# Conditioning map of a four-layer diffusion step: where its two sums are formed, and beside which sub-layers

## The chip, the cores and the metric

The kernel runs on one core of a Trainium2 chip. The metric is device time in microseconds (us) of one execution; lower is better. The engines are the tensor engine (PE; PEld is its weight load), the vector engine (DVE), the scalar engine (ACT), GpSimd (POOL) and SyncE (SP), which issues the loads.

## What is computed

One step of a backbone of four layers over 128 context tokens and 512 latent tokens of 1024 channels, all in fp32. Each layer has a token mixer (latent attention, centred pooling, grouped 2-D Fourier, short gated convolution) and a gated ConvFFN. Both sub-layers are modulated by six vectors (shift, scale, gate) that come from a conditioning map:

```python
mod = jax.nn.silu(cond) @ P["ada_w"][li] + P["ada_b"][li]      # cond: c or c_ctx; ada_w: 1024 x 6144 per layer
sh1, sc1, g1, sh2, sc2, g2 = jnp.split(mod, 6, axis=-1)
h = _modulate(_rmsnorm(x, P["norm1_w"][li]), sh1, sc1)
x = x + g1[:, None, :] * mixer(h)
h = _modulate(_rmsnorm(x, P["norm2_w"][li]), sh2, sc2)
x = x + g2[:, None, :] * _conv_ffn(h, ...)
```

There are two conditioning vectors (one for context, one for latent tokens), so the map of a layer is a 2 x 1024 by 1024 x 6144 product whose 25 MB of weights are used once.

## The kernel before

Activations lie with channels on partitions: `x` is eight chunks of 128 channels by 640 tokens. Every fp32 product is three products of rounded parts (`wh`/`wl` for a weight and its rest, `XH`/`XL` or `hh`/`hl` for the operand). A weight comes as a 128 x 1024 tile (`wraw`), ACT casts it to `wh` (L184), DVE subtracts to get `wl` (L185). `mm3` (L225) then runs 48 matmuls of about 320 columns into a wide PSUM tile `mm`, of which there are two. In an FFN a unit is such a tile of weights: 44 products up and 24 down, in thirds. After a pair of products up, DVE evacuates both PSUM tiles (`ev`, L391), applies two taps of the convolution (`gc`, L412 and L413), forms `hd` (L452, L453) and its rest `hl` (L402). After a product down, DVE updates `x` (L362, L363).

The map is worked on in tiles of 128 input channels by 1024 outputs; a layer has 48, eight for a group of 1024 outputs, 192 in all. `ada_step` (L128) does one tile: it loads up to the pool's number of tiles ahead, but not past `ada["cap"]`, and then multiplies in one of two ways.

- **Direct** (where `ada["early"]` is None): four matmuls of the tile itself (`adaraw`) with the conditioning vectors as stationary operand (L160).
- **Sums** (where `ada["early"]` is a pool): the products are summed over the eight channel chunks beside the tensor engine, into two tiles `adasum` (`a0`, `a1`) of 128 x 1024, one per conditioning vector. After the eighth tile, eight small matmuls (L160, `pick`) add over the partitions. Then DVE transposes (L163) and adds the offset (L167).

Before, the tiles go so. Layer 0: 16 direct tiles at the start, one group of eight as sums in the projections (`three`, `krope`, `kv`), eight direct in `latent_keys`, 16 direct in the heads (one per stage of the 41 in `heads`). Layer 1: 48 as sums in FFN 0. Layer 2: 24 direct in the pooling mixer (three after each chunk, `proj` in `pool`), 24 as sums in FFN 1. Layer 3: 48 as sums in FFN 2. FFN 3 has none. An FFN calls `ada_step` after each unit up from the third on and after each product down of the first two thirds (58 calls).

Each engine runs its instructions in the order in which the framework's scheduler placed them when the program was built; a waiting instruction holds all that stand behind it on its engine. SP issues weight tiles and map tiles from one queue.

Of the kernel before, what the change touches and what calls it, by code (L numbers as in the profile page):

```python
# [13 lines left out]
ALU = mybir.AluOpType  # L14
# [40 lines left out]
# column offsets in the array of small per-channel vectors  # L55
# [18 lines left out]
def build(tc, a, plan=None):  # L74
# [53 lines left out]
    def ada_step(limit):  # L128
        i = ada["done"]
        end = min(limit, DEPTH) * 48  # L130
# [11 lines left out]
        if ada["sums"]:  # L142
            # the products summed over the channel chunks beside the tensor engine
            c_, (a0, a1) = [cond_s[:, k, r : r + 1] for r in range(2)], ada["sums"]
            if k == 0:
                V.tensor_scalar(a0, raw, c_[0], None, ALU.mult)
                S.activation(a1, raw, AF.Copy, scale=c_[1])
            else:
                V.scalar_tensor_tensor(a0, raw, c_[0], a0, ALU.mult, ALU.add)  # L149
                S.activation(raw, raw, AF.Copy, scale=c_[1])  # L150
                G.tensor_tensor(a1, a1, raw, ALU.add)  # L151
            todo = [(pick[:, r], acc, r == 0, r == 1) for r, acc in enumerate(ada["sums"])] if k == 7 else []
        else:
            todo = [(condz[:, k], raw, k == 0, k == 7)]
# [39 lines left out]
    def prefetch(upto):  # L194
        """emit the loads of the units up to the given count of weight units, but none beyond a barrier"""
# [27 lines left out]
    def mm3(o, wh, wl, mh, ml, n, bias, m=P, mid=None, apart=False):  # L223
        """o (token columns 192:832, bias columns 190:192) = sum over n chunks of w[k].T @ moving[k];
        mid: functions to call after a chunk; apart: the two banks one after the other"""  # L225
# [20 lines left out]
    st = dict(xh=None, xl=None, ssum=None, rstd=None, rB=None, xap=None, xstack=None)  # L246

    def norm_scale(l, which, lo):
        """per-channel factor norm_w * (1 + scale) of both condition vectors, four chunks"""
# [25 lines left out]
    def norm_prep(d, nxt):  # L275
        """after chunk d of x is final: its squares, and the modulated operand of sub-layer nxt = (layer, which)"""
        norm_sq(d, nxt is None)
        if nxt is not None:
            norm_xa(d, nxt)
# [41 lines left out]
    def rms_a(ssum, n, pool=None, rest=None):  # L321
        """rstd of the five token tiles, one value per partition"""
# [18 lines left out]
    def rms_b(r, pool=None, bufs=2):  # L341
        """rstd along the free dimension of every partition"""
# [45 lines left out]
    def evac(o, m=P):  # L388
        """psum * rstd with the two bias columns in front"""
# [15 lines left out]
    def conv3(gp, cols, bias):  # L405
        """three taps over the padded row (zeros at 0, 129, 642); outputs at 0:128 and 129:641"""
# [14 lines left out]
    def ffn(l, nxt):  # L421
# [49 lines left out]
        # a third of the products down follows the first products up of the next third  # L471
# [10 lines left out]
    def mla(nxt):  # L482
# [4 lines left out]
        def start():  # L487
# [18 lines left out]
            ada["cap"] = 32  # L506
# [43 lines left out]
        def take(dst, *parts):  # L550
            """normalise a projection, add its shift; parts: psum pieces, the two bias columns first"""
# [13 lines left out]
        def three(wh, wl):  # L565
            """the first three projections at once: their first four channel chunks while the shifts and scales of
            the others are still under way"""
# [15 lines left out]
            with tc.manual_schedule(engines={mybir.EngineType.PE}):  # L583
# [3 lines left out]
                ada["early"] = st["nb"]  # L587
# [9 lines left out]
                more(2)  # L597
# [4 lines left out]
            more(2)  # L602
# [13 lines left out]
        def krope(wh, wl):  # L616
            o = psum_mm()
            mm3(o, wh, wl, st["xh"], st["xl"], KC, True, m=96)
            more(2)
# [14 lines left out]
        def kv(i):  # L634
            def fn(wh, wl):
                o = psum_mm()
                mm3(o, wh, wl, st["xh"], st["xl"], KC, True, mid=None if i else {0: latent_q_stats, 4: latent_q})
                more(1)
# [5 lines left out]
        def heads_start():  # L644
            # the projections of the tokens are done: their operands make room for the heads
# [7 lines left out]
        def latent_keys():  # L653
            ada["early"] = None
            more(1)
# [5 lines left out]
            more(7)  # L661
# [11 lines left out]
        def heads_pools():  # L673
# [3 lines left out]
            ada["cap"] = 48  # L677
# [11 lines left out]
        # ---- the heads: scores of one query block beside the values of the block before, other  # L689
        # products in between ----  # L690
# [8 lines left out]
        def product(wh, wl, mh, ml, n, halves, post):  # L699
            """one output chunk, a half of the moving columns (one psum bank) at a time"""  # L700
# [100 lines left out]
        def combine(dst, o, n, hh, cols):  # L801
            """the two halves of the value operand: o[0:64] + o[64:128]"""
# [5 lines left out]
        class Block:  # L808
            """256 queries of one head"""
# [62 lines left out]
        class Context:  # L872
            """the prompt's own queries and keys, two heads"""
# [85 lines left out]
        def heads():  # L959
# [7 lines left out]
            # products to fit in beside the blocks: (first stage, weights, pieces, number of pieces)  # L967
# [30 lines left out]
            def fill(stage, k):  # L998
                """the next k pieces of the items open at this stage"""
# [25 lines left out]
            for i in range(len(blocks) + 1):  # L1025
# [4 lines left out]
                if i % nst == 0 and i:  # L1030
                    # the operands of the next pair must stand
# [105 lines left out]
    def pool(nxt):  # L1137
# [7 lines left out]
        def start():  # L1145
# [11 lines left out]
            cell["ada"] = ada["pool"], ada["bufs"]  # L1157
            ada["pool"], ada["bufs"], ada["cap"] = cell["pool"], 5, 2 * 48 + 24

        def finish():  # L1160
            ada["pool"], ada["bufs"] = cell["ada"]
            ada["cap"] = DEPTH * 48
            ctx.close()
# [35 lines left out]
        def proj(g):  # L1199
            def fn(wh, wl):  # L1200
# [7 lines left out]
                for i in range(2):  # L1208
                    finish_chunk(2 * g + i, cell["o"].pop(0))
                    for _ in range(3):  # L1210
                        ada_step(l + 2)
# [16 lines left out]
    def fourier(nxt):  # L1228
# [21 lines left out]
        def table(dst_h, dst_l, src):  # L1250
            """a constant table in its two parts"""
# [15 lines left out]
        def shift():  # L1267
            # the shift is constant over time: it reaches only the zero frequency
# [382 lines left out]
```

## Time and profile before

| | |
|---|---|
| runs | 2812.65, 2810.16, 2804.65 us; median 2810.16 |
| span of the profiled execution, first to last instruction | 2811.5 us; no separate time is given for it |
| PE busy | 2712.0 us (96%) |
| DVE busy | 1802.0 us (64%) |
| ACT busy | 1158.7 us (41%) |
| POOL busy | 549.6 us (20%) |

The page gives busy time by engine, the chain of waits that ended last, and groups of instructions. A share over the whole span is a mean over stages with different limits, so the trace is read by stage: windows (busy time in a stretch), waits (who waited for whom) and timelines (instructions in order of time).

### The profile page before, as it was taken

The page shows a single profiled execution, that of the slowest core. Times are in us where ns is not written, and L with a number is a line of the kernel's source. Part 1 is how long each engine was busy: PE and PEld are TensorE (multiplying, and loading weights), DVE is VectorE, ACT ScalarE, POOL GpSimd, SP SyncE. Part 2 cuts the span into 40 slices and gives each one's busy share as a digit, 9 for nine tenths or more (in the row PEclk, how much of TensorE's full clock was granted, in tenths as well). Part 3 has the DMA queues.
Part 4 walks back from the last instruction along what each step waited for, and adds up shares of the span by engine and source line. Part 5 has one row for each costly group of instructions (what it writes and reads, how often), then busy time and mean ns, then how long its engine had stood idle before and what let it go on. Part 6 is the DMA issues. An engine that isn't in the chain of part 4 may idle for free.

```text
span 2811.5 us, 44335 instructions
## 1 busy us (share of the span) xinstructions
PE 2712.0 (96%) x18417; PEld 2614.4 (93%) x18417; DVE 1802.0 (64%) x2354; ACT 1158.7 (41%) x1693; POOL 549.6 (20%) x328
## 2 busy tenths in 40 slices
PE   7999999999999889999999999999999999999998
PEld 5788989999999779999998999999999999999998
DVE  5778888877855888644454688686555555535353
ACT  4566665434433444332333354343332233313231
POOL 3222323422320333200012133332010010000001
PEclk9999999999999999999999999999999999999998
DMA  7431113443432544312221244433122221222221
GB/s 286 133 103 44 44 35 104 154 141 135 128 107 70 186 156 148 116 68 75 75 69 56 91 150 143 150 133 123 64 79 75 76 76 69 75 76 72 79 71 58
DMA packets 85656, 287.69 MB, mean 102 GB/s; under 512 B 10880, under 2 KB 13872, under 8 KB 85456
## 3 DMA queue, kind: packets, MB, share of 16 engines
q1 hardware_dynamic: 84816, 284.44, 30.0%
q8 instruction: 145, 2.38, 0.3%
q14 instruction: 55, 0.45, 0.1%
q10 hardware_dynamic: 288, 0.25, 0.0%
q0 software_dynamic: 352, 0.17, 0.0%
HBM read 279.42 MB, written 2.77 MB: 100 GB/s over the span
## 4 chain that ended last, share of the span: by engine, by line
PE 74%; DVE 14%; issue 5%; ACT 3%; DMA 2%; POOL 2%; SPq 0%; POOLq 0%; DVEq 0%; ACTq 0%
PE mm L235 62%; DVE adasum L149 4%; PE smp L708 3%; DVE wl L185 2%; DMA adaraw<-in_ada_w 2%; POOL adasum L151 2%; PE mm L823 1%; PE smp L845 1%; DVE ev L391 1%; DVE hl L402 1%; PE mm L1320 1%; PE adaacc L160 1%; DVE XL L312 1%; PE smp L861 1%; PE smp L754 1%
## 5 line engine op out<-in xcount | busy, mean ns | idle before, releaser
L235 PE MATMUL mm<-XH,wh 128*128 128x322 f32 (+1 forms) x3280 | 765.6, 315 | 34.1 <-DVE ev L391 29.2
L235 PE MATMUL mm<-XH,wl 128*128 128x322 f32 (+1 forms) x3280 | 760.8, 313 | 5.8 <-DVE wl L185 5.8
L235 PE MATMUL mm<-XL,wh 128*128 128x322 f32 (+1 forms) x3280 | 760.7, 313 | 1.5 <-DVE XL L312 1.5
L184 ACT CAST wh<-wraw 128x1024 fp32r<-128x1024 f32 (+4 forms) x355 | 348.4, 983 | 756.2 <-PE mm L235 639.7
L235 PEld LDWEIGHTS mm<-XH,wh 128*128 128x128 f32 (+1 forms) x3280 | 557.3, 191 | 45.9 <-issue 26.2
L235 PEld LDWEIGHTS mm<-XH,wl 128*128 128x128 f32 (+1 forms) x3280 | 558.4, 190 | 8.7 <-DVE wl L185 7.1
L235 PEld LDWEIGHTS mm<-XL,wh 128*128 128x128 f32 (+1 forms) x3280 | 558.6, 191 | 6.5 <-issue 4.5
L185 DVE TENSOR_TENSOR wl<-wraw,wh 128x1024 fp32r<-128x1024 f32 (+2 forms) x335 | 444.9, 1328 | 67.6 <-ACT wh L184 66.8
L151 POOL TENSOR_TENSOR adasum<-adasum,adaraw 128x1024 f32<-128x1024 f32 x112 | 318.9, 2847 | 559.5 <-ACT adaraw L150 555.9
L391 DVE TENSOR_TENSOR ev<-mm,rB 128x642 f32<-128x642 f32 x208 | 171.2, 824 | 341.5 <-PE mm L235 335.2
L235 PE MATMUL mm<-hh,wh 128*128 128x320 f32 x1536 | 349.9, 309 | 4.0 <-DVE x L363 4.0
L235 PE MATMUL mm<-hh,wl 128*128 128x320 f32 x1536 | 349.3, 309 | 0.0
L235 PE MATMUL mm<-hl,wh 128*128 128x320 f32 x1536 | 349.3, 309 | 0.0
L291 POOL TENSOR_TENSOR ssum<-ssum,sq 128x640 f32<-128x640 f32 x54 | 91.9, 1702 | 1315.6 <-ACT sq L287 1310.6
L235 PEld LDWEIGHTS mm<-hh,wh 128*128 128x128 f32 x1536 | 256.0, 188 | 7.2 <-issue 5.1
L235 PEld LDWEIGHTS mm<-hh,wl 128*128 128x128 f32 x1536 | 256.5, 188 | 0.0
L235 PEld LDWEIGHTS mm<-hl,wh 128*128 128x128 f32 x1536 | 256.3, 188 | 0.0
L149 DVE SCALAR_TENSOR_TENSOR adasum<-adaraw,condz,adasum 128x1024 f32<-128x1024 f32 x112 | 224.2, 2002 | 13.9 <-DMA adaraw<-in_ada_w 13.2
L362 DVE SCALAR_TENSOR_TENSOR x<-mm,mod,x 128x128 f32<-128x128 f32 x112 | 39.1, 349 | 295.1 <-PE mm L235 295.1
L150 ACT ACTIVATE adaraw<-adaraw,condz 128x1024 f32<-128x1024 f32 x112 | 129.0, 1153 | 212.7 <-DVE adasum L149 140.9
L401 ACT CAST hh<-hd 128x640 fp32r<-128x640 f32 x96 | 69.8, 727 | 186.5 <-DVE hd L453 168.8
L402 DVE TENSOR_TENSOR hl<-hd,hh 128x640 fp32r<-128x640 f32 x96 | 94.5, 984 | 59.2 <-ACT hh L401 59.2
(296 smaller groups left out, 3241.1 us busy)
## 6 DMA issues: line engine op xcount, KB each, us to landing
adaraw<-in_ada_w SPq DMA_DIRECT2D x192, 512.0 KB, 3.6
wraw<-in_ffn_up SPq DMA_DIRECT2D x176, 512.0 KB, 3.2
wraw<-in_ffn_dn SPq DMA_DIRECT2D x64, 448.0 KB, 3.2
wraw<-in_ffn_dn SPq DMA_DIRECT2D x32, 512.0 KB, 3.2
wraw<-in_sconv_win SPq DMA_DIRECT2D x24, 512.0 KB, 3.2
wraw<-in_wo SPq DMA_DIRECT2D x8, 512.0 KB, 3.3
wraw<-in_fnet_w SPq DMA_DIRECT2D x8, 512.0 KB, 3.2
wraw<-in_sconv_wout SPq DMA_DIRECT2D x8, 512.0 KB, 3.2
```

Of the source, the lines that this page charges most:

```text
L149: V.scalar_tensor_tensor(a0, raw, c_[0], a0, ALU.mult, ALU.add)
L150: S.activation(raw, raw, AF.Copy, scale=c_[1])
L151: G.tensor_tensor(a1, a1, raw, ALU.add)
L184: S.copy(h[:, :n], raw[:, :n])
L185: (eng or V).tensor_tensor(lo[:, :n], raw[:, :n], h[:, :n].bitcast(F32), ALU.subtract)
L235: TE.matmul(o[:m, c0:c1], w_[:, k], x_[k][:, x0 : x0 + c1 - c0], start=st, stop=sp)
L291: (G if d < KC - 1 else V).tensor_tensor(st["ssum"], st["ssum"], sq, ALU.add)
L362: V.scalar_tensor_tensor(x[:, d, 0:TP], o[:, lo : lo + TP], g[:, 0:1], x[:, d, 0:TP], ALU.mult, ALU.add)
L391: V.tensor_tensor(t[:m], o[:m, 190:832], st["rB"][:m], ALU.mult)
L401: S.copy(h, v)
L402: V.tensor_tensor(lo, v, h.bitcast(F32), ALU.subtract)
L708: TE.matmul(o[:, 0 : c1 - c0], w_[:, k], x_[k][:, c0:c1], start=st_, stop=sp)
```

## The change

Two things. First, both sums are formed by DVE: ACT's scaling (L147, L150) and POOL's addition (L151) of the second sum become a second `tensor_scalar` or `scalar_tensor_tensor` on DVE. Second, the tiles move. Projections and `latent_keys`: none any more (cap 16). Heads: 24 direct tiles, up to a cap of 40. FFN 0: 56 as sums (the last eight of layer 0, which hold the gate of FFN 0, and all of layer 1). Pooling mixer: none. FFN 1: 48 as sums. FFN 2: 48 as sums, as before. Direct tiles are 40 instead of 64, tiles as sums 152 instead of 128. Comments and docstrings are emptied too, so that line numbers in the changed kernel are lower by two to four behind L151 (by ten in the heads).

```diff
 def ada_step(limit):
-        end = min(limit, DEPTH) * 48
+        end = min(min(limit, DEPTH) * 48, ada["cap"])
...
-            if k == 0:
-                V.tensor_scalar(a0, raw, c_[0], None, ALU.mult)
-                S.activation(a1, raw, AF.Copy, scale=c_[1])
-            else:
-                V.scalar_tensor_tensor(a0, raw, c_[0], a0, ALU.mult, ALU.add)
-                S.activation(raw, raw, AF.Copy, scale=c_[1])
-                G.tensor_tensor(a1, a1, raw, ALU.add)
+            for r, a_ in enumerate((a0, a1)):
+                if k == 0:
+                    V.tensor_scalar(a_, raw, c_[r], None, ALU.mult)
+                else:
+                    V.scalar_tensor_tensor(a_, raw, c_[r], a_, ALU.mult, ALU.add)
...
 def mla(nxt):            # start
-            ada["cap"] = 32
+            ada["cap"] = 16
...                       # three, krope, kv, latent_keys
-                ada["early"] = st["nb"]
-                more(2)
-            more(2)
-            more(2)
-                more(1)
-            ada["early"] = None
-            more(1)
-            more(7)
...                       # heads_pools
-            ada["cap"] = 48
+            ada["cap"] = 40
...
 def pool(nxt):
-            cell["ada"] = ada["pool"], ada["bufs"]
-            ada["pool"], ada["bufs"], ada["cap"] = cell["pool"], 5, 2 * 48 + 24
-            ada["pool"], ada["bufs"] = cell["ada"]
-            ada["cap"] = DEPTH * 48
-                    for _ in range(3):
-                        ada_step(l + 2)
...
         def ensure(l=l, nxt=nxt, s_=s_):
-            while ada["done"] < (l + 1) * 48 and (l, s_) != (0, "mix"):
+            need = 0 if (l, s_) == (0, "mix") else 40 if (l, s_) == (0, "ffn") else (l + 1) * 48
+            while ada["done"] < need:
                 ada_step(l + 1)
```

The scheduler places the instructions anew. Three places show it.

The vector engine in FFN 0, at the start of the second group of eight tiles there (`adasum` are the sums, `ev` the evacuations, `wl` the splits of weights), before:

```order
L146 TENSOR_SCALAR adasum<-adaraw,condz 128x1024
L255 SCALAR_TENSOR_TENSOR nscale<-mod_82,sm 128x4 x2
L149 SCALAR_TENSOR_TENSOR adasum<-adaraw,condz,adasum 128x1024
L402 TENSOR_TENSOR hl<-hd,hh 128x640
L149 SCALAR_TENSOR_TENSOR adasum<-adaraw,condz,adasum 128x1024 x2
L391 TENSOR_TENSOR ev<-mm,rB 128x642
L185 TENSOR_TENSOR wl<-wraw,wh 128x1024
L149 SCALAR_TENSOR_TENSOR adasum<-adaraw,condz,adasum 128x1024
L412 SCALAR_TENSOR_TENSOR gc<-gp,conv,gc 128x641
L149 SCALAR_TENSOR_TENSOR adasum<-adaraw,condz,adasum 128x1024
L413 SCALAR_TENSOR_TENSOR gc<-gp,conv,gc 128x641
```

and now:

```order
L147 TENSOR_SCALAR adasum<-adaraw,condz 128x1024 x2
L400 TENSOR_TENSOR hl<-hd,hh 128x640
L149 SCALAR_TENSOR_TENSOR adasum<-adaraw,condz,adasum 128x1024 x3
L183 TENSOR_TENSOR wl<-wraw,wh 128x1024
L389 TENSOR_TENSOR ev<-mm,rB 128x642
L149 SCALAR_TENSOR_TENSOR adasum<-adaraw,condz,adasum 128x1024 x2
L410 SCALAR_TENSOR_TENSOR gc<-gp,conv,gc 128x641
L149 SCALAR_TENSOR_TENSOR adasum<-adaraw,condz,adasum 128x1024
L411 SCALAR_TENSOR_TENSOR gc<-gp,conv,gc 128x641
L389 TENSOR_TENSOR ev<-mm,rB 128x642
L183 TENSOR_TENSOR wl<-wraw,wh 128x1024
```

Each tile now has two instructions here. The group's sixteen are spread over five units of the FFN, where the eight of before stood in about three; the evacuations and splits keep their order.

The vector engine in the projections, behind the modulation of the last channels (`ev` the evacuations of the first projections, `ss` their sum of squares), before:

```order
L185 TENSOR_TENSOR wl<-wraw,wh 128x768
L556 TENSOR_TENSOR ev<-mm,rB 128x642
L149 SCALAR_TENSOR_TENSOR adasum<-adaraw,condz,adasum 128x1024
L556 TENSOR_TENSOR ev<-mm,rB 128x642
L185 TENSOR_TENSOR wl<-wraw,wh 128x1024
L149 SCALAR_TENSOR_TENSOR adasum<-adaraw,condz,adasum 128x1024 x2
L544 TENSOR_TENSOR ss<-ss,ssq 128x640
L556 TENSOR_TENSOR ev<-smp,rB 128x322
L556 TENSOR_TENSOR ev<-smp,rB 128x320
```

and now:

```order
L183 TENSOR_TENSOR wl<-wraw,wh 128x768
L554 TENSOR_TENSOR ev<-mm,rB 128x642 x2
L183 TENSOR_TENSOR wl<-wraw,wh 128x1024
L542 TENSOR_TENSOR ss<-ss,ssq 128x640
L554 TENSOR_TENSOR ev<-smp,rB 128x322
L554 TENSOR_TENSOR ev<-smp,rB 128x320
L183 TENSOR_TENSOR wl<-wraw,wh 128x1024
```

The map's instructions between the evacuations and the sum of squares are gone.

The tensor engine in the keys of the attention (`qH` the last query product, `ident` the broadcast of the statistics, `kH`/`kL` the first value products), before:

```order
L708 MATMUL smp<-qH,wl 128x320
L160 MATMUL adaacc<-adaraw,condz 32x256 x4
L349 MATMUL smp<-ident,rstd 128x128 x3
L160 MATMUL adaacc<-adaraw,condz 32x256 x5
L349 MATMUL smp<-ident,rstd 128x128 x2
L160 MATMUL adaacc<-adaraw,condz 32x256 x7
L754 MATMUL smp<-wh,kH 128x256
L754 MATMUL smp<-wh,kL 128x256
```

and now:

```order
L698 MATMUL smp<-qH,wl 128x320
L347 MATMUL smp<-ident,rstd 128x128 x5
L744 MATMUL smp<-wh,kH 128x256
L744 MATMUL smp<-wh,kL 128x256
L744 MATMUL smp<-wl,kH 128x256
```

The direct tiles that stood between the statistics and the value products are gone; they stand in the heads now.

## Rows read from the trace of the kernel before

**Rows 1.** Windows of FFN 0 to 3: stretch, length, busy per engine.

```profile
core 0: us, PE busy (x) PEld busy (x) DVE busy (x) ACT busy (x) POOL busy (x), PEclk, DMA share, GB/s
446.40:938.80 492.40, 480.39 (x3267) 472.88 (x3266) 355.16 (x371) 211.89 (x257) 134.62 (x61) 1.00 0.37 121
1009.00:1482.40 473.40, 466.20 (x3144) 462.33 (x3144) 291.14 (x325) 181.00 (x225) 71.16 (x28) 0.99 0.28 94
1595.20:2091.90 496.70, 484.44 (x3286) 477.64 (x3285) 354.45 (x362) 209.55 (x253) 131.94 (x49) 0.99 0.36 121
2321.40:2792.50 471.10, 471.10 (x3194) 471.10 (x3193) 214.81 (x274) 150.14 (x188) 10.58 (x7) 1.00 0.20 69
```

**Rows 2.** Tile adasum: durations in ns, min/median/max.

```profile
L149 DVE SCALAR_TENSOR_TENSOR adasum<-adaraw,condz,adasum x112: 1268/1285/3428, 44.7 to 1941.2; 128x1024 f32<-128x1024 f32 x112
L151 POOL TENSOR_TENSOR adasum<-adasum,adaraw x112: 2363/2872/3481, 48.3 to 1944.8; 128x1024 f32<-128x1024 f32 x112
L146 DVE TENSOR_SCALAR adasum<-adaraw,condz x16: 741/749/751, 43.5 to 1919.1; 128x1024 f32<-128x1024 f32 x16
```

**Rows 3.** Timeline in FFN 0: start, duration, engine, line, operation.

```profile
494.61 2.82 POOL L151 TENSOR_TENSOR adasum<-adasum,adaraw 128x1024 f32<-128x1024 f32 x1 [2.47 <-ACT adaraw L150]
495.09 3.43 DVE L149 SCALAR_TENSOR_TENSOR adasum<-adaraw,condz,adasum 128x1024 f32<-128x1024 f32 x1
499.24 0.81 DVE L391 TENSOR_TENSOR ev<-mm,rB 128x642 f32<-128x642 f32 x1
```

**Rows 4.** Waits of the tensor engine in FFN 2: total us, times, longest.

```profile
PE mm L235 <- DVE ev L391: 8.4, 4, 2.2
```

**Rows 5.** Two short windows, columns as in rows 1.

```profile
74.00:81.00 7.00, 6.60 (x27) 6.60 (x28) 5.77 (x9) 3.05 (x7) 3.78 (x3) 0.52 0.56 187
500.00:504.50 4.50, 4.30 (x19) 4.34 (x20) 4.14 (x5) 2.19 (x4) 2.26 (x1) 0.62 0.29 85
```

**Rows 6.** Vector engine groups, FFN 2: busy us, mean ns, idle before.

```profile
L185 DVE TENSOR_TENSOR wl<-wraw,wh 128x1024 fp32r<-128x1024 f32 (+1 forms) x68 | 98.5, 1448 | 16.2 <-ACT wh L184 16.2
L149 DVE SCALAR_TENSOR_TENSOR adasum<-adaraw,condz,adasum 128x1024 f32<-128x1024 f32 x42 | 83.8, 1994 | 5.9 <-DMA adaraw<-in_ada_w 5.7
```

**Rows 7.** The same view of FFN 3.

```profile
L185 DVE TENSOR_TENSOR wl<-wraw,wh 128x1024 fp32r<-128x1024 f32 (+1 forms) x66 | 78.5, 1189 | 3.4 <-ACT wh L184 3.4
```

**Rows 8.** Window: the first 18 products up of FFN 3.

```profile
2321.40:2451.90 130.50, 130.50 (x886) 130.50 (x885) 68.17 (x84) 51.15 (x68) 1.18 (x1) 1.00 0.21 73
```

**Rows 9.** Timeline, start and projections, vector and tensor engine.

```profile
44.66 1.28 DVE L149 SCALAR_TENSOR_TENSOR adasum<-adaraw,condz,adasum 128x1024 f32<-128x1024 f32 x1
70.25 3.35 DVE L149 SCALAR_TENSOR_TENSOR adasum<-adaraw,condz,adasum 128x1024 f32<-128x1024 f32 x1
73.53 0.81 DVE L544 TENSOR_TENSOR ss<-ss,ssq 128x640 f32<-128x640 f32 x1
74.40 0.80 PE L328 MATMUL smp<-ones,ss 128*128 128x1 f32 x3 [5.72 <-DVE ss L544]
```

**Rows 10.** Timeline of the tensor engine, latent keys.

```profile
93.13 1.07 PE L160 MATMUL adaacc<-adasum,pick 128*32 128x256 f32 x16
98.20 1.25 PE L328 MATMUL smp<-ones,ss 128*128 128x1 f32 x10 [1.17 <-DVE ss L544]
102.12 0.64 PE L160 MATMUL adaacc<-adaraw,condz 128*32 128x256 f32 x8
102.69 0.93 PE L349 MATMUL smp<-ident,rstd 128*128 128x128 f32 x6
109.38 0.39 PE L754 MATMUL smp<-wh,kL 128*128 128x256 f32 x1 [0.35 <-DVE kL L525]
```

**Rows 11.** Windows of the pooling mixer and the heads.

```profile
944.00:1008.60 64.60, 49.56 (x365) 33.74 (x365) 59.39 (x103) 25.53 (x46) 25.15 (x16) 0.87 0.65 227
120.70:432.50 311.80, 305.01 (x2091) 267.79 (x2089) 250.16 (x506) 200.58 (x438) 87.25 (x104) 1.00 0.20 61
```

**Rows 12.** DMA issues: KB each, median us from issue to landing.

```profile
adaraw<-in_ada_w SPq DMA_DIRECT2D x192, 512.0 KB, 3.6
```

## The prediction

> **What bounds the kernel now.** I read the windows first. FFN 3, which carries no tile of the map, shows PE busy for all of its 471.1 us. FFN 0 and FFN 2 run the same products and take 492.4 and 496.7 us [rows 1]. So the tensor engine is the bound, and the map beside it is what an FFN loses time to: 21.3 us in FFN 0 and 25.6 us in FFN 2. PE's idle time there is length less busy: 12.0, 7.2 and 12.3 us in FFN 0, 1 and 2 [rows 1]. The waits say on whom: most of FFN 2's is four waits of about 2.1 us on DVE's evacuation `ev` [rows 4]. Each stop also costs clock: in the 4.5 us from 500.0 the granted clock is 0.62 in the mean, part of it at 1.2 instead of 2.4 GHz, which loses 1.7 us [rows 5].
>
> Why is `ev` late? The groups and the timeline tell. A `scalar_tensor_tensor` of the map takes 1.285 us in the median but up to 3.428 [rows 2], 1.994 in the mean of FFN 2 [rows 6]. The long one at 495.09 began 0.48 us after POOL's addition had begun and lasted until about 1.1 us after that ended: POOL until 497.43, then a full run of DVE's own 1.27 [rows 3]. So the two do not share; DVE waits POOL's addition out. Other DVE work pays too: a split of a weight takes 1.448 us in the mean of FFN 2 and 1.189 in FFN 3 [rows 6, 7], 17.6 us over 68. DVE is thus 71% busy in FFN 2, part of it waiting for POOL, and its queue, which is in order, brings `ev` too late now and then.
>
> **The change, term by term.** The sum is made against the span of 2811.5 us; the median of the runs is 2810.16, 0.05% away, so nothing is corrected between them.
>
> *FFN 2* has 48 tiles before and after. Removed: 42 + 6 instructions of ACT, 42 additions of POOL. Added: 42 `scalar_tensor_tensor` at 1.285 and 6 `tensor_scalar` at 0.749 on DVE [rows 2], 58 us. Given back: 42 times (1.994 less 1.285), 30 us, and the 18 us of the splits [rows 6, 7], with more on smaller lines. So DVE stays near its 354 us of about 480. What decides is its order within a group of eight tiles. In the new order the group's 14 + 2 instructions stand in five units. A unit is 7.25 us long (130.5 us for 18), and DVE's own work in it without the map is 3.79 us (68.17 by 18) [rows 8]. Five units need 5 x 3.79 + 14 x 1.285 + 2 x 0.749 = 38.4 us where PE gives 36.3. `ev` comes up to 2.2 us late, and it may be 6.4 late (a unit less the 0.81 of `ev` itself [rows 3]), because there are two PSUM tiles. So the waits should go. Splits stand one to two units ahead of use and have more room. Bounds: none of the waits goes (0), all go with their clock. I take the second less 1 us, since 2.2 of 6.4 is nearest to no wait: FFN 3's 471.1, six groups of small matmuls at 1.07 [rows 10], and 1, which is 478.5: **-18.2 us**.
>
> *FFN 0* has 56 tiles, seven groups: 471.1 + 7.5 + 2 (about 1 us of its waits is at its start, on the modulation, and stays) = 480.6: **-11.8 us**. The group that moved here is the layer's own last gate; it is used first by the products down after nine pairs, and its eight calls are over after five.
>
> *FFN 1* has 48 for 24. Of its 7.2 us of idle time [rows 1] I keep 1.5; a half-clock stretch of the kind above goes (1.7); three more groups cost 3 x 1.07 on PE: **-4.2 us**. The 24 more loads of 512 KB [rows 12] bring its DMA share from 0.28 to about FFN 0's and FFN 2's 0.37 [rows 1]; there, in FFN 2, DVE waited 5.7 us in all for tiles to land [rows 6].
>
> *Start and projections.* The sums leave. In the start, one instruction of 1.28 us stood among the modulations that PE waits for [rows 9]; with its follow-ups I take **-2** (0 to -3). In the projections PE stopped 5.72 us for a sum of squares at 73.53, right behind a map instruction of 3.35 us [rows 9]; then came a half-clock stretch, 0.52 over 7 us, 3.4 us lost [rows 5]. Without the map the sum stands directly behind its evacuation, several us before PE wants it: **-9.1** (0 to -9.1). The group's small matmuls, 1.07 us at 93.13, filled time before a wait of 1.17 at 98.20 [rows 10]: worth nothing, the wait grows. SP's queue loses 16 tile loads that stood between those of the weights; these can only come earlier.
>
> *Latent keys and heads.* Eight direct tiles go from one to the other. One costs PE 0.57 us (102.12 to 102.69 [rows 10]), eight 4.6. In the heads PE is busy 98% of 311.8 us [rows 11], so they cost +4.6. In the latent keys they partly filled a chain (statistics, broadcast, keys) whose end PE already waited for at 109.38 [rows 10]; leaving saves 3.5, the pieces that delayed the broadcast and those behind it, at least 0 and at most 4.6. Net **+1** (0 to +4.6). In SP's queue the loads stand among those of query rows as they did for 16 tiles.
>
> *Pooling mixer.* 24 direct tiles leave, some 13 us of PE. But DVE is the bound: busy 59.4 of 64.6 us, PE 49.6 [rows 11], much of that PE time being these tiles. What leaves DVE is three transposes and three additions, about 3 us. PE then idles more, and the clock, 0.87 already [rows 11], may fall. I take **-2** (-4 to +5). SP's 24 tile loads no longer stand before those of FFN 1.
>
> Sum: -18.2 - 11.8 - 4.2 - 2 - 9.1 + 1 - 2 = -46.3, so **2765 us**.
>
> **The rivals.** *Another wait takes its place.* DVE may wait for tiles to land (5.7 us in FFN 2 [rows 6]) and then be late on top of 2.2; each tile is now held until two DVE instructions have read it. For it: three buffers only, and SP's queue, where a tile's load can stand behind a weight's that waits for its own buffer. Against it: 4 us more are free. If half of the waits of the FFNs (15 us) and of their clock (4) stay: 2784.
>
> *The cover is missed.* PE's filling tiles leave the keys and the mixer, the 3.5 us there become idle time, and the clock stays low into FFN 1, some 10 us at half rate: +3.5 + 5, so 2774. For it: the mixer's clock of 0.87 with the tiles in place [rows 11]. Against: PE is not what the mixer waits for. The Trainium skill, TensorE: Matmul & The Clock Gate (Part 1), says that the throttled state is the default and that activity releases it. By that rule this case is the likelier one; the trace agrees in so far as 74 to 81 is at 0.52 after a stop.
>
> *DVE becomes the bound* (slower). If the instruction costs its mean of 1.994 us [rows 6] for a reason other than POOL, five units need 19.0 + 1.5 + 27.9 = 48.4 us, `ev` is 12.1 late, and PE stops 5.7 us plus 1.7 of clock. 13 of the 19 groups begin in products up: 13 x 7.4 = 96, and 2765 becomes about 2860. It decides from (36.3 + 6.4 - 20.5) / 14 = 1.58 us on. Against: the median of 1.285 is nearly the minimum of 1.268 [rows 2], so whatever lengthens it comes and goes, and rows 3 name it. The Trainium skill, Perfetto Trace Analysis (Optimizing Scalar/DVE Operations), says that a busy DVE may be relieved by moving work to ACT or even GpSimd. By that rule the change is the wrong way round; in this trace the relief costs DVE as much as it takes off.
>
> *Nothing to measure.* The gains are eaten elsewhere, for instance by a worse order in the heads, where 1% is 3 us: 2805.
>
> **How the numbers follow.** Forecast 0.65, with its own bounds from 2744 (start, mixer and keys at their best, no residue in the FFNs) to 2778. Another wait 0.15, cover missed 0.10, nothing 0.05, DVE bound 0.05. The range is 2744 to 2792: it takes in the first three and some spread of the second. A measurement of this kernel can tell about 0.3%, 8.4 us. Faster by more than that is all below 2802: 0.90; same 0.05; slower 0.05.
>
> **What would show it.** Right: no POOL work on `adasum`; the map's `scalar_tensor_tensor` at 1.27 to 1.30 us nearly without spread; splits of FFN 2 near 1.19; FFN 0 about 481 us, FFN 2 about 478, with PE waiting for `ev` under 2 us; no stop at the sum of squares and no half clock around 74. The pooling mixer within 3 us of its 64.6. Wrong: a mean of the map's instruction above 1.58; waits of PE on `ev` as many as before; waits of DVE on landing tiles above 10 us in an FFN; heads longer by over 8 us; a mixer that grows.

## The result, and the profile after

The changed kernel takes 2768.44 us in the median (2767.82 to 2769.44, four runs), the kernel before 2808.25 us beside it (2804.65 to 2812.65). The ratio is 0.9847 with a 95% interval of 0.9833 to 0.9861. The forecast was 2765 (2744 to 2792). The profiled execution of the changed kernel spans 2767.4 us, that of before 2811.5. The forecast takes 46.3 us from that span; by the medians the change gains 39.8, by the two profiled executions 44.0.

Windows of FFN 0 to 3 in the changed kernel, which answer to [rows 1]: stretch, length, busy time of PE, PEld, DVE, ACT and POOL with instructions, granted clock, DMA share, GB/s.

```profile
442.20:920.80 478.60, 477.92 (x3282) 471.79 (x3282) 357.31 (x437) 160.87 (x209) 14.52 (x19) 1.00 0.41 133
990.00:1459.60 469.60, 469.26 (x3196) 464.12 (x3196) 333.55 (x403) 155.60 (x201) 11.72 (x7) 0.99 0.38 122
1571.00:2048.80 477.80, 477.80 (x3286) 473.13 (x3285) 338.09 (x410) 158.46 (x205) 11.67 (x7) 1.00 0.39 125
2278.40:2749.20 470.80, 470.80 (x3192) 470.80 (x3190) 214.68 (x273) 150.04 (x188) 10.57 (x7) 1.00 0.21 69
```

PE is now busy for the whole of FFN 2 and for all but 0.7 us of FFN 0. DVE does twice as many instructions of the map and is not busier for it: 338 us in FFN 2 after 354.

The map's sums in the whole kernel (least, median and longest duration in ns, first and last start), as [rows 2]:

```profile
L149 DVE SCALAR_TENSOR_TENSOR adasum<-adaraw,condz,adasum x266: 1269/1278/1289, 469.6 to 1900.1; 128x1024 f32<-128x1024 f32 x133
L147 DVE TENSOR_SCALAR adasum<-adaraw,condz x38: 742/748/752, 468.3 to 1878.0; 128x1024 f32<-128x1024 f32 x38
```

DVE's groups in FFN 2 (busy us, mean ns, idle before), as [rows 6]:

```profile
L149 DVE SCALAR_TENSOR_TENSOR adasum<-adaraw,condz,adasum 128x1024 f32<-128x1024 f32 x84 | 104.1, 1276 | 0.0
L183 DVE TENSOR_TENSOR wl<-wraw,wh 128x1024 fp32r<-128x1024 f32 (+1 forms) x68 | 80.7, 1186 | 4.0 <-ACT wh L182 3.8
```

The spread is gone: the longest instruction of the map is 1.289 us, where it was 3.428, and the splits of FFN 2 take 1186 ns, those of FFN 3 1189 [rows 7]. No wait of DVE for a landing tile is left in front of the map's instructions.

The next table compares the two executions stage by stage. A stage runs from its first matmul on PE to that of the next, so the lengths add up to the span. FFN 0 begins with its own first product, while the last products of the attention still run; the mixer, FFN 1, FFN 2 and the short convolution begin with the matmuls of their statistics. Each length is that of one execution: with the same instructions the keys take 24.0 to 25.6 us and the pooling mixer 63.9 to 66.0 in the executions of this document.

| stage, us | before | after | change | forecast |
|---|---|---|---|---|
| start | 60.5 | 57.8 | -2.7 | -2 |
| projections | 33.6 | 23.6 | -10.0 | -9.1 |
| latent queries and keys | 24.2 | 24.3 | +0.2 | -3.5 |
| heads | 314.2 | 322.4 | +8.2 | +4.6 |
| FFN 0 | 509.4 | 495.6 | -13.7 | -11.8 |
| pooling mixer | 66.3 | 65.6 | -0.7 | -2 |
| FFN 1 | 474.3 | 470.2 | -4.0 | -4.2 |
| Fourier mixer | 117.3 | 115.8 | -1.5 | 0 |
| FFN 2 | 496.6 | 477.8 | -18.8 | -18.2 |
| short convolution, FFN 3 | 715.1 | 714.1 | -0.9 | 0 |
| sum | 2811.5 | 2767.4 | -44.0 | -46.3 |

The three FFNs and the projections gave 46.5 us. The latent keys and the heads together gave back 8.4 where +1 was forecast. The timeline of PE in the projections and keys (start, duration, line, operation, in brackets the idle time and its releaser) shows both:

```profile
65.83 1.17 PE L326 MATMUL smp<-ones,ss 128*128 128x1 f32 x10
85.59 1.25 PE L326 MATMUL smp<-ones,ss 128*128 128x1 f32 x10 [1.34 <-DVE ss L542]
91.46 0.38 PE L744 MATMUL smp<-wh,kH 128*128 128x256 f32 x1 [0.76 <-ACT rB L350]
95.00 0.50 PE L744 MATMUL smp<-wh,kH 128*128 128x256 f32 x2 [1.85 <-ACT kH L522]
97.01 0.58 PE L744 MATMUL smp<-wh,kL 128*128 128x256 f32 x1 [1.51 <-DVE kL L523]
```

The stop of 5.72 us at the first sum of squares [rows 9] is gone. But without the direct tiles the keys now wait three times, 4.1 us in all, and after that the clock fell. Windows of the keys, the heads and the mixer:

```profile
95.00:104.00 9.00, 7.49 (x37) 7.29 (x38) 5.21 (x10) 2.89 (x7) 1.01 (x3) 0.62 0.42 143
105.80:428.20 322.40, 315.61 (x2166) 271.25 (x2167) 253.67 (x515) 201.04 (x441) 87.38 (x105) 1.00 0.24 72
926.00:990.00 64.00, 36.40 (x172) 33.65 (x172) 55.02 (x97) 25.74 (x46) 27.87 (x16) 0.76 0.17 59
```

In the keys the granted clock is 0.62 in the mean, part of it at 1.2 GHz. That is no accident of one execution: in all eight profiled kernels without tiles in the keys the clock falls at 94 to 98 us, for some 7 us, and in none of the five with them does it fall there. The mixer keeps its length with 13 us less of PE's time and a clock of 0.76 after 0.87 [rows 11]. The same stretch of the heads in the kernel before, from the first score to the first product of FFN 0:

```profile
118.30:432.50 314.20, 307.33 (x2104) 268.93 (x2103) 251.98 (x513) 202.22 (x441) 88.24 (x105) 1.00 0.20 62
```

So the heads' 8.2 us are work of PE (315.6 busy after 307.3), not waits. The timeline of PE beside two of the eight added tiles:

```profile
235.33 0.28 PE L850 MATMUL smp<-ph,vt 128*128 128x256 f32 x1
235.54 0.62 PE L158 MATMUL adaacc<-adaraw,condz 128*32 128x256 f32 x2
236.09 0.38 PE L851 MATMUL smp<-pl,vt 128*128 128x256 f32 x1
...
237.19 0.63 PE L158 MATMUL adaacc<-adaraw,condz 128*32 128x256 f32 x6
237.76 0.39 PE L812 MATMUL mm<-KH,qph 96*128 96x256 f32 x1
```

A tile has eight records (two for each of its four matmuls). It is cut in two here, and the piece of two records takes as long, 0.55 us to the next start, as that of six, 0.57, or as the whole tile in [rows 10], 0.57. The eight added tiles stand in 13 pieces more than before (35 for 22). 13 x 0.56 is 7.3 us, and the matmul behind a piece starts its successor about 0.1 us late, another 1.3: 8.6 by this estimate, for 8.2 measured.

### The profile page after: what moved, and what is told of

Its sections match the earlier page's. It is cut to its first block, busy times and chain, and to the rows that moved or that the text cites. A ratio compares the mean times of both kernels' runs of the same rounds, so it can differ in the third digit from the quotient of the medians.

```text
span 2767.4 us, 43800 instructions
## 1 busy us (share of the span) xinstructions
PE 2690.0 (97%) x18273; PEld 2607.3 (94%) x18273; DVE 1805.3 (65%) x2530; ACT 1022.1 (37%) x1565; POOL 231.8 (8%) x216
## 4 chain that ended last, share of the span: by engine, by line
PE 92%; DVE 4%; ACT 2%; issue 1%; POOL 1%; DMA 0%; SPq 0%; POOLq 0%; DVEq 0%; ACTq 0%
PE mm L233 78%; PE smp L698 3%; PE adaacc L158 2%; PE mm L813 1%; PE smp L835 1%; PE mm L1304 1%; PE smp L851 1%; PE smp L850 1%; PE mm L812 1%; PE smp L744 1%; DVE XL L310 1%; PE smp L347 0%; PE smp L326 0%; POOL win L1168 0%; PE mm L578 0%
## 5 line engine op out<-in xcount | busy, mean ns | idle before, releaser
L233 PE MATMUL mm<-XH,wh 128*128 128x322 f32 (+1 forms) x3280 | 762.3, 314 | 26.0 <-DVE ev L389 11.6
L183 DVE TENSOR_TENSOR wl<-wraw,wh 128x1024 fp32r<-128x1024 f32 (+2 forms) x335 | 396.7, 1184 | 41.9 <-ACT wh L182 39.9
L149 DVE SCALAR_TENSOR_TENSOR adasum<-adaraw,condz,adasum 128x1024 f32<-128x1024 f32 x266 | 330.0, 1278 | 0.0
L410 DVE SCALAR_TENSOR_TENSOR gc<-gp,conv,gc 128x641 f32<-128x641 f32 x88 | 78.0, 886 | 61.8 <-ACT gc L409 61.8
L310 DVE SCALAR_TENSOR_TENSOR XL<-x,nscale,XH 128x128 fp32r<-128x128 f32 (+1 forms) x128 | 113.2, 905 | 5.1 <-ACT XH L309 3.5
L447 ACT ACTIVATE gc<-gc 128x641 f32<-128x641 f32 x88 | 65.3, 742 | 134.4 <-DVE gc L411 133.4
```

The source lines that it names most:

```text
L149: V.scalar_tensor_tensor(a_, raw, c_[r], a_, ALU.mult, ALU.add)
L183: (eng or V).tensor_tensor(lo[:, :n], raw[:, :n], h[:, :n].bitcast(F32), ALU.subtract)
L233: TE.matmul(o[:m, c0:c1], w_[:, k], x_[k][:, x0 : x0 + c1 - c0], start=st, stop=sp)
L310: V.scalar_tensor_tensor(lo[:, 2 + c0 : 2 + c1], x[:, d, c0:c1], s_, h[:, 2 + c0 : 2 + c1].bitcast(F32), ALU.mult, ALU.subtract)
L410: V.scalar_tensor_tensor(gc, gp[:, 0:641], cols[:, 0:1], gc, ALU.mult, ALU.add)
L447: S.activation(gc, gc, AF.Gelu)
```

## The experiments

The theory is that of the forecast: a vector instruction with two operands in SBUF waits out an addition of POOL, that makes `ev` late, and forming both sums on DVE ends it. The rivals: the moves of the tiles gained, or ACT's relief, or the end of the chain from tile to ACT to POOL. Times are medians; "before" beside the first four was 2810.36 us, beside the next four 2808.11, beside the last three 2811.00.

| stage, us | before | after | sums alone | moves alone | POOL adds | keys | mixer | both |
|---|---|---|---|---|---|---|---|---|
| projections to keys | 57.8 | 48.0 | 52.1 | 47.6 | 48.0 | 51.2 | 49.0 | 48.4 |
| heads | 314.2 | 322.4 | 314.1 | 322.4 | 322.5 | 314.1 | 322.4 | 314.1 |
| FFN 0 | 509.4 | 495.6 | 498.5 | 512.3 | 510.8 | 495.6 | 495.7 | 496.4 |
| pooling mixer | 66.3 | 65.6 | 66.0 | 65.2 | 64.1 | 64.2 | 66.3 | 66.2 |
| FFN 1 | 474.3 | 470.2 | 465.5 | 484.4 | 483.0 | 470.2 | 466.4 | 465.2 |
| FFN 2 | 496.6 | 477.8 | 477.8 | 492.1 | 492.6 | 477.8 | 477.8 | 477.8 |

### The sums alone, and the moves alone

First run: in the kernel before, the lines of the two sums are replaced by those of the change, and no tile moves.

```diff
-                S.activation(raw, raw, AF.Copy, scale=c_[1])
-                G.tensor_tensor(a1, a1, raw, ALU.add)
+            for r, a_ in enumerate((a0, a1)):
...
+                    V.scalar_tensor_tensor(a_, raw, c_[r], a_, ALU.mult, ALU.add)
```

> The kernel before with one edit: both sums are formed by the vector engine; every tile of the map stays beside the sub-layer where it was. Theory (the addition on POOL is what made the vector engine late): FFN 2 shortens as in the changed kernel, by about 19 us, FFN 0 with 48 tiles by 14, FFN 1 with 24 by about 5, and the sums that stay in the projections no longer take up to 3.4 us, which gives 4 (0 to 9). 2808 - 42 = 2766 us (2760 to 2772), no map instruction above 1.30 us. Rival (moving the tiles is what gained): at least 2795 us.

Measured: 2764.79 us, ratio 0.9834 (0.9812 to 0.9857). The second run takes the changed kernel and undoes this edit; the tiles stay where the change put them.

> The changed kernel with the second sum back on ACT and POOL; the tiles stand where the change put them. Theory (the addition on POOL is the cost): start and projections keep their gain, 12.7 us, the heads keep their loss, 8.4; FFN 0 carries seven groups for six and loses 3 more than before, FFN 1 carries six for three and loses 10 to 24 more, FFN 2 is as before. 2808 - 4 + 13 to 27 = 2817 to 2831 us, the map's scalar_tensor_tensor at about 2 us in the mean of FFN 2. Rival (the moves gained): 2770 to 2795 us.

Measured: 2815.44 us, ratio 1.0020 (1.0009 to 1.0031). DVE's groups in its FFN 2:

```profile
L185 DVE TENSOR_TENSOR wl<-wraw,wh 128x1024 fp32r<-128x1024 f32 (+1 forms) x68 | 98.6, 1450 | 17.6 <-ACT wh L184 17.6
L149 DVE SCALAR_TENSOR_TENSOR adasum<-adaraw,condz,adasum 128x1024 f32<-128x1024 f32 x42 | 83.9, 1999 | 5.3 <-DMA adaraw<-in_ada_w 5.0
```

These are the means of [rows 6] again. So the sums are the whole gain: alone they are 3.7 us below the changed kernel (the two were not timed beside each other, and the intervals of their ratios overlap), and the moves alone make the kernel 5 us slower. FFN 1 shows why: with POOL's addition, 48 tiles for 24 cost it 10 us more, the lower end of what was expected of this run; without, 470.2 against 465.5. The whole time of the moves alone was missed from below, 2815.4 for 2817 to 2831: FFN 2, expected as before, is 4.5 us shorter. PE idles in it as long as before (12.5 us for 12.3) but is busy for 479.6 us instead of 484.3, at a granted clock of 1.00 instead of 0.99: the waits came back, the half-clock stretches behind them did not. The sums alone have a longer FFN 0 than the changed kernel, 498.5 us with 48 tiles for 495.6 with 56; in its first 50 us the granted clock is 0.90, in the changed kernel 0.97.

### Is it POOL, or the chain? An addition that nobody reads

In the changed kernel POOL adds each tile to itself after both sums have read it. Nobody reads the result.

```diff
+            k and G.tensor_tensor(raw, raw, raw, ALU.add); ...
```

> The changed kernel with one addition more on POOL per tile of the map worked on as sums (k > 0): the tile is added to itself in place after both sums have read it, and nobody reads the result. No instruction of the vector engine depends on it, apart from the tile's buffer, which comes free some 3 us later. Theory (a vector instruction with two operands in SBUF waits out an addition of POOL): the map's scalar_tensor_tensor is at 1.7 to 2.3 us in the mean again with a maximum above 3, the splits of FFN 2 above 1.3, the tensor engine waits for the evacuations; 2800 to 2840 us. Rival (the length came from the chain tile, ACT, POOL that the sums waited in): 2766 to 2772 us, mean 1.28.

Measured: 2812.71 us, ratio 1.0005 (0.9995 to 1.0014): one instruction per tile that no result depends on takes back the whole gain. Tile views of its sums and its additions, PE's largest wait, and, last, the same wait in the changed kernel:

```profile
L149 DVE SCALAR_TENSOR_TENSOR adasum<-adaraw,condz,adasum x266: 1268/1274/2918, 469.0 to 1942.1; 128x1024 f32<-128x1024 f32 x133
L150 POOL TENSOR_TENSOR adaraw<-adaraw x133: 1894/2812/4008, 471.5 to 1945.2; 128x1024 f32<-128x1024 f32 x133
...
PE mm L233 <- DVE ev L389: 21.6, 13, 5.6
...
PE mm L233 <- DVE ev L389: 11.6, 4, 5.6
```

Nearly all of the 11.6 us lies in the pooling mixer. In the FFNs it is not `ev` alone that comes late: there PE waits 10.3 us for `ev`, 12.5 for `gc` (ACT's Gelu behind DVE's taps) and 10.4 for DVE's update of `x`, where the changed kernel has 0.3 us on `ev` in FFN 1 and nothing on the other two.

The timeline of POOL and DVE at the first of them shows the lock with its own control:

```profile
471.54 2.47 POOL L150 TENSOR_TENSOR adaraw<-adaraw 128x1024 f32<-128x1024 f32 x1 [21.14 <-DVE adasum L149]
472.17 0.82 DVE L389 TENSOR_TENSOR ev<-mm,rB 128x642 f32<-128x642 f32 x1
472.91 2.18 DVE L183 TENSOR_TENSOR wl<-wraw,wh 128x1024 fp32r<-128x1024 f32 x1
```

Both vector instructions begin while POOL adds (until 474.01). `ev` has one operand in PSUM and takes its usual 0.82. The split has two in SBUF: it takes 2.18, which is POOL's rest of 1.10 and most of its own 1.19. Over the whole run, by the starts and ends in the trace, the map's instruction takes 2.67 us in the mean of the 55 that begin during an addition and 1.27 in the 144 that no addition touches; splits 2.01 (73) and 1.18; `ev` 0.81 (41) and 0.83. In FFN 2 the expected mean of 1.7 to 2.3 was missed from below (1.57), since DVE has twice the instructions to spread one addition over; the time was as expected.

The Trainium skill, SBUF — State Buffer (SBUF: two separate sides), states this lock: a vector instruction with two inputs in SBUF and a GpSimd instruction that reads SBUF exclude each other for a whole instruction. The trace agrees for the addition, in the rows just shown, and from POOL's side too: the 22 additions that begin while no such vector instruction runs take 1.89 us, the 111 that begin within one 2.35 or more. The next two runs ask what POOL has to do for it.

### Which work of POOL does it?

In place of the addition, POOL multiplies the tile by a scalar (one operand read), or fills it with zeros (none read).

```diff
+            k and G.tensor_scalar(raw, raw, c_[0], None, ALU.mult); ...
...
+            k and G.memset(raw, 0.0); ...
```

> As the run with POOL's addition of the tile to itself, but POOL multiplies the tile by a scalar in place: one operand of 128 x 1024 for two. Theory A (any work of POOL that reads SBUF keeps out vector instructions with two operands in SBUF): such vector instructions that begin during it wait it out again; how much it costs goes by POOL's duration, and if that is 1 to 2 us for 2.8, the time is 2780 to 2805 us. Theory B (only an addition with two operands does it): 2766 to 2772 us, the map's instruction at 1.28 us without spread.

> The same place, but POOL fills the tile with zeros: it writes as many bytes and reads none. Theory A (what counts is that POOL reads): 2766 to 2773 us, the map's instruction at 1.28 us without spread. Theory B (any access of POOL to SBUF does it): longer in proportion to the fill's duration, 2775 to 2805 us, with maxima of the map's instruction above 2 us.

Measured: 2768.62 us, ratio 0.9850 (0.9835 to 0.9865), for the scalar; 2769.42 us, 0.9853 (0.9837 to 0.9870), for the fill. Tile views, the scalar's run first, then the fill's:

```profile
L150 POOL TENSOR_SCALAR adaraw<-adaraw,condz x133: 2842/3365/4902, 472.8 to 1905.9; 128x1024 f32<-128x1024 f32 x133
L149 DVE SCALAR_TENSOR_TENSOR adasum<-adaraw,condz,adasum x266: 1268/1274/2164, 470.2 to 1902.0; 128x1024 f32<-128x1024 f32 x133
```

```profile
L150 POOL MEMSET adaraw<- x133: 952/956/964, 470.6 to 1899.9; 128x1024 f32 x133
L149 DVE SCALAR_TENSOR_TENSOR adasum<-adaraw,condz,adasum x266: 1271/1278/1289, 468.1 to 1898.5; 128x1024 f32<-128x1024 f32 x133
```

The fill leaves no mark at all, though 15 instructions of the map begin during one: theory A of that run. For the scalar both theories fall. POOL is busy for longer than with the addition, 3.4 us a tile, and yet the 122 instructions of the map that begin during it take 1.40 us in the mean, 0.13 above the others, with a longest of 2.16. Its timeline at the same place:

```profile
472.81 3.43 POOL L150 TENSOR_SCALAR adaraw<-adaraw,condz 128x1024 f32<-128x1024 f32 x1 [21.16 <-DVE adasum L149]
473.43 0.82 DVE L389 TENSOR_TENSOR ev<-mm,rB 128x642 f32<-128x642 f32 x1
474.17 1.41 DVE L183 TENSOR_TENSOR wl<-wraw,wh 128x1024 fp32r<-128x1024 f32 x1
```

The split ends at 475.58, 0.66 before POOL does. So POOL's instruction with one operand does not keep the vector engine out for its whole length. The "whole instruction" of the Trainium skill, SBUF — State Buffer (SBUF: two separate sides), does not hold for it here. Instead POOL pays: a scaling that begins while no vector instruction with two operands in SBUF runs takes 2.85 us (29 of them), the other 104 take 3.91 in the mean. Why it gives way was not tried.

### ACT's part

ACT's scaling of the tile is put back, in place and unread.

```diff
+            k and S.activation(raw, raw, AF.Copy, scale=c_[1]); ...
```

> The changed kernel with ACT's scaling of the tile put back, in place after both sums have read it; nobody reads the result. It holds the tile's buffer about 1 us longer. Theory (ACT had no part in the gain): 2766 to 2773 us, the map's scalar_tensor_tensor at 1.28 us. Rival (ACT's relief, or tiles that come free earlier, gave a good part of it): 2780 us or more, with the casts of the weights late or the vector engine waiting for tiles to land.

Measured: 2769.87 us, ratio 0.9855 (0.9836 to 0.9874); FFN 0, 1 and 2 at 495.6, 470.0 and 477.8, as without it. ACT had no part in the gain. Nor had the time for which a tile is held: POOL's scaling held it for longer than POOL's addition, and the gain stayed.

### How much room DVE has

A third `scalar_tensor_tensor` per tile, into the tile's own buffer and unread.

```diff
+            k and V.scalar_tensor_tensor(raw, raw, c_[0], a0, ALU.mult, ALU.add); ...
```

> The changed kernel with a third scalar_tensor_tensor of 128 x 1024 on the vector engine per tile worked on as sums (k > 0), into the tile's own buffer; nobody reads the result. It adds 133 x 1.28 = 170 us of vector work, 63 us in FFN 0. Theory A (the slack is counted over the five units in which a group stood): a group needs 5 x 3.79 + 21 x 1.28 + 1.5 = 47.3 us where the tensor engine gives 36.3 and allows 6.4 more, so each of 19 groups stops it for 4.6 us and some clock: 2840 to 2880 us. Theory B (the order spreads a group over seven or eight units, 7 x 7.25 = 50.8 us for 7 x 3.79 + 28.4 = 54.9, 4.1 late of 6.4): 2768 to 2785 us.

Measured: 2771.17 us, ratio 0.9866 (0.9852 to 0.9881). FFN 2 is 1.0 us longer, FFN 0 and 1 by 1.0 and 0.7. DVE in FFN 0, and PE's one wait in FFN 2:

```profile
447.40:924.20 476.80, 476.10 (x3272) 470.33 (x3271) 411.61 (x481) 158.22 (x205) 12.10 (x16) 1.00 0.40 130
...
PE mm L233 <- DVE ev L389: 0.8, 1, 0.8
```

DVE is 86% busy there and PE does not wait. Theory B: the scheduler spreads a group over more units when it grows. In FFN 0 and 2 a group's instructions of the map span 39 to 54 us, in the changed kernel 24 to 37.

### The places that the tiles left

Eight direct tiles go back into the latent keys (16 in the heads for 24); 24 go back into the pooling mixer (24 sums in FFN 1 for 48); both.

```diff
 def heads_start():
+            ada["cap"] = 24; [ada_load() for _ in range(20 - ada["load"])]
...
 def latent_keys():
-            rB = rms_b(c["rk"], c["raw"], 1)
+            more(1); rB = rms_b(c["rk"], c["raw"], 1)
...
+                split(c["kH"][j][:, PAST:], c["kL"][j][:, PAST:], ck); j and more(7)
...
 def pool(nxt):
...
+            cell["ada"] = ada["pool"], ada["bufs"]; ada["pool"], ada["bufs"], ada["cap"] = cell["pool"], 5, 2 * 48 + 24
...
+            ada["pool"], ada["bufs"] = cell["ada"]; ada["cap"] = DEPTH * 48
...
+                    finish_chunk(2 * g + i, cell["o"].pop(0)); [ada_step(l + 2) for _ in range(3)]
```

> The changed kernel with eight direct tiles of layer 0 back in the latent keys, 16 instead of 24 in the heads; the first four are loaded as the projections end. Theory (a direct tile costs the tensor engine about 1.05 us among the blocks of the heads, since each piece that it is split into takes 0.55 us however small; in the keys it stands in time that is waited away): heads 8 us shorter, keys from 1 longer to 3 shorter; 2760 us (2757 to 2763). Rival (the heads are longer for another reason, or what leaves them comes back in the keys): 2766 to 2770 us.

> The changed kernel with 24 direct tiles of layer 2 back in the pooling mixer, 24 instead of 48 as sums in FFN 1. Theory (the mixer waits for the vector engine whether or not the tensor engine has tiles to fill with; in FFN 1 a group costs its eight small matmuls): mixer within 1 us of 65.6, FFN 1 4 to 5 shorter through three groups less and a clock that does not start low; 2764 us (2762 to 2767). Rival (the mixer gains from the tiles that left it): 2769 us or more.

> Both edits of the two runs before: eight direct tiles in the latent keys, 24 in the pooling mixer, no sums in the projections, 56, 24 and 48 tiles as sums in FFN 0, 1 and 2. Theory (the two places do not touch each other): 2756 us (2753 to 2760), faster than the kernel before, the changed kernel, and the sums alone (2764.8). Rival (one place gives back what the other gains): 2763 to 2768 us.

Measured: 2761.78 us, ratio 0.9833 (0.9818 to 0.9848), with the keys; 2766.07, 0.9848 (0.9832 to 0.9865), with the mixer; 2759.34, 0.9824 (0.9810 to 0.9839), with both. Each is inside its expected range. The heads give back all of their 8.3 us. In the mixer the tiles cost some 1.4 us (65.4 to 66.3, mean 66.0, in the five executions with them; 63.9 to 66.0, mean 64.7, in the eight without), in FFN 1 three groups less save 4 to 6. Both edits together run in 2756.98 to 2760.88 us, below all runs of the changed kernel (2767.82 to 2769.44) and of the kernel before, though the two were not timed beside each other and the intervals of their ratios touch.

One point was missed: with the keys alone, queries and keys are 3.3 us longer, not 1 longer to 3 shorter. The windows of the same 8 us in that run and in the run with both, which has the same instructions here:

```profile
85.00:93.00 8.00, 7.74 (x37) 6.63 (x38) 5.05 (x12) 4.16 (x8) 2.35 (x3) 0.57 0.18 47
...
85.00:93.00 8.00, 8.00 (x71) 5.96 (x71) 7.25 (x13) 5.18 (x10) 3.15 (x3) 1.00 0.33 72
```

In both PE had just waited 1.3 us for a sum of squares. In the one part of the stretch then ran at 1.2 GHz (0.57 in the mean), in the other none.

### Fewer pieces in the heads

On top of both edits, two tiles after every second stage of the heads for one after each.

```diff
-                ada_step(1)
+                i % 2 and (ada_step(1), ada_step(1))
```

> The kernel with eight direct tiles in the latent keys and 24 in the mixer, and in the heads two tiles after every second stage instead of one after each: the 16 tiles stand in 15 pieces for 22. Theory (a piece of one to four matmuls costs the tensor engine 0.55 us, one of five to eight 1.0, and 0.1 to 0.2 for its neighbours): pieces 13.2 to 11.4 us, neighbours 7 x 0.15, so 3 us less than 2759.3: 2756 us (2754 to 2758). Rival (time goes by the number of matmuls, which is the same): 2759 to 2761 us.

Measured: 2755.59 us (2754.17 to 2763.01), ratio 0.9809 (0.9792 to 0.9825). The time is what the theory expected, though its runs overlap with those without pairs (2756.98 to 2760.88), and the stage is not: the heads are 315.5 us, 1.5 longer than without pairs, and the gain lies in the Fourier mixer, FFN 1 and other stages whose code is the same. The window behind the first pair, and its pieces:

```profile
112.00:120.00 8.00, 7.96 (x50) 5.13 (x48) 4.25 (x9) 3.47 (x8) 0.91 (x1) 0.77 0.37 134
...
112.07 1.06 PE L158 MATMUL adaacc<-adaraw,condz 128*32 128x256 f32 x2
113.90 1.91 PE L158 MATMUL adaacc<-adaraw,condz 128*32 128x256 f32 x14
```

To the next start the first pair's two pieces took 0.99 and 1.84 us where later pieces of 2 and 14 records take 0.55 and 0.99, and the clock is 0.77 behind it. All 15 pieces together took 12.7 us, the 22 of the run with both edits 14.1; with the first pair at the later price it would be 11.4, what the theory had. So the price of a piece holds. Whether the stage would gain at full clock is open.

## Why the prediction was right

**What bounds the kernel, and why `ev` is late.** Right, and shown: POOL's addition alone, without any dependency, brings the waits back (on `gc` and `x` as much as on `ev`); ACT and the tile's holding time do not matter; the sums alone give the gain.

**FFN 2 and FFN 0.** -18.2 and -11.8 were forecast, -18.8 and -13.7 came. FFN 3's length plus 1.07 us for each group of small matmuls was the right sum: 470.8 + 6 x 1.07 = 477.2 against 477.8. The 1 and 2 us that were kept for residual waits were not needed: in FFN 0, 0.7 us of waits are left.

**FFN 1.** -4.2 forecast, -4.0 measured. The one price that could be isolated, three groups at 3.2 us, measured 3.8 to 5.8 (470.2 less 464.4 to 466.4). Two misses cancel inside the -4.0. Idle time fell to 0.3 us, not 1.5. But the clock's 1.7 us did not come: the first 8 us of FFN 1 now run at 1.2 GHz. Here they are in the changed kernel, then in the kernel before:

```profile
989.40:997.40 8.00, 7.66 (x33) 7.18 (x33) 2.96 (x5) 3.19 (x6) 1.18 (x1) 0.50 0.00 0
...
1008.10:1016.10 8.00, 7.17 (x43) 6.84 (x42) 4.56 (x6) 4.50 (x7) 1.18 (x1) 0.79 0.01 2
```

Its price is some 2 us as an estimate: of two executions with the mixer's 24 tiles in place, one with this start at full clock has an FFN 1 of 464.4 us (pairs), one with most of it at half 466.4 (mixer).

**Start and projections.** -11.1 forecast, -12.7 measured. With the tiles left there and the sums on DVE alone, projections and keys gain 5.7 of the 9.8 us: the rest is the move's.

**Latent keys and heads: the step that failed.** "One costs PE 0.57 us, eight 4.6" took the price of a whole tile from [rows 10]. Among the blocks of the heads tiles are cut, and a cut tile pays 0.55 us for each piece. The trace of before showed it: its 16 tiles of the heads already stood in 22 pieces. The other half, "leaving saves 3.5", fell too: the rival of the missed cover came true in the keys. The chain there (broadcast, keys, their rest) takes as long without the tiles, PE waits 4.1 us for it, and here the clock fell. Together +8.4 for +1. One of the forecast's own signs of being wrong, heads longer by over 8 us, came with it.

**Pooling mixer.** -2 forecast with -4 to +5, -0.7 measured. PE's clock and busy time fell, as the rival said, and the mixer did not grow by it: PE is not its bound. The low clock did reach into FFN 1, as the rival said too, at some 2 us for its 5. The Trainium skill, TensorE: Matmul & The Clock Gate (Part 1), says that activity releases the throttle. The trace agrees: with less work on PE the mixer is throttled more, 0.76 after 0.87.

**DVE as the bound.** Rightly given 0.05, but its point of decision, 1.58 us an instruction, was far too low. The third instruction per tile puts 21 x 1.28 + 1.5 = 28.4 us into a group, as much as 14 instructions of 1.92 us would, and nothing stops: the five units were a property of the order found for 16 instructions, not a limit, and only of some of its groups: the 24 to 37 us of the changed kernel are as long as three to five units of 7.25. The Trainium skill, Perfetto Trace Analysis (Optimizing Scalar/DVE Operations), which the forecast cited for relieving a busy DVE, also warns that GpSimd and DVE share a port and that moving work between them might not help. The forecast left that half out; it is the half that the run with POOL's unread addition shows.

The total is right because the terms that carry it were. That the sum came within 3.4 us of the median owes something to luck: FFN 0, the start, the projections and the Fourier mixer together gained 5 us more than forecast, against 7 lost in the heads and keys and 1 in the pooling mixer. As a gain, 46.3 us were forecast and 39.8 measured by the medians; about 3 us of the difference are the base: the sum was made from the span of 2811.5, the median of before is 2808.25.

## What to carry to other kernels

Before giving work to POOL beside a busy DVE, count what two-operand additions there do to vector instructions whose operands both lie in SBUF: here such an instruction waited up to 2.2 us, and taking the relief back made the kernel 1.7% faster (0.9834, 0.9812 to 0.9857). Look for it as a spread between median and maximum in one group, and check by the durations of those that begin during POOL's work, with an operation that reads PSUM as control. A small matmul squeezed between others is priced by its pieces, read at the place where it will stand; and a time that comes out as expected has to be found again in the stage that the theory names.

## What was not expected of the hardware

- An instruction of POOL with one operand (3.4 us a tile) delayed an instruction of the map that began during it by 0.13 us in the mean, one with two operands (2.8 us a tile) by 1.4. POOL's own wait is part of both: where no vector instruction with two operands in SBUF runs as they begin, they take 2.85 and 1.89.
- A piece of direct tile takes PE 0.55 to 0.57 us for two, six or eight records and 1.0 for 14 or 16.
- After the same wait of 1.3 us and before the same instructions the granted clock was 0.57 over 8 us in one execution and 1.00 in another, a difference of some 3 us in stages of 25.
